# First loads of a two-layer encoder: x in blocks of 128 columns, idle products in two lists, a planner that knows two rings

## The chip, the core and the metric

The kernel runs on one core of a Trainium2 chip. The metric is device time in microseconds (us) from launch to the end of the program, taken over several runs. A core has engines that work side by side, each through its own list of instructions: TensorE (PE; PEld is its loading of stationary operands), VectorE (DVE), ScalarE (ACT), GpSimd (POOL) and SyncE (SP). SyncE and ScalarE also issue the transfers between HBM and the on-chip memory SBUF; TensorE writes its products to PSUM. An engine takes its instructions strictly in the order in which they stand, and waits at one until the semaphores that it names have come.

## What is computed

Two layers of a transformer encoder on 256 tokens of width 1024, in float32. Each layer normalises x, projects it (2560 columns), attends in three groups of heads (neighbourhood, dilated, grouped-query), normalises and projects back, and then runs a gated feed-forward part with a short convolution over tokens. Cut to what matters here (the first projection is [256, 1024] by [1024, 2560]; DEPTH is 2; q and k are normalised per head and rotated before the three attentions):

```python
def mixer_sublayer(x, n1, w_in_l, qg, kg, rpb_l, og, w_out_l, tables):
    h = rms_norm(x, n1)
    proj = h @ w_in_l
    qa, ka, va, qd, kd, vd, qc, kc, vc = jnp.split(proj, cuts, axis=-1)
    ...
    mix = jnp.concatenate([rms_norm(out_a, ...), rms_norm(out_d, ...), rms_norm(out_c, ...)], axis=-1)
    return x + mix @ w_out_l

def channel_sublayer(x, n2, w_gu, cw, cb, w_dn):
    h = rms_norm(x, n2)
    g, u = jnp.split(h @ w_gu, 2, axis=-1)
    g = depthwise_conv_centred(g, cw, cb)
    return x + (jax.nn.gelu(g, approximate=False) * u) @ w_dn

def reference(x, ...):
    for l in range(DEPTH):
        x = mixer_sublayer(x, ...)
        x = channel_sublayer(x, ...)
    return x
```

## The kernel before, in words

Products in full precision are made from halves: an operand is split into a high part (rounded to the TensorE's fast float format, `fp32r`) and a low part (what is left), and three products hi·hi, hi·lo, lo·hi are added in PSUM (`mm3`). ScalarE makes the high part (a CAST to `wp_hi`), VectorE the low part (a subtraction to `wp_lo`).

**Weights** come in units (`units_of`), each a transfer from HBM into one of four raw buffers (`wp_raw`). `load` issues it, `split` halves it. Units 0 and 1 belong to the first projection of layer 1 (dq, 384 columns): unit 0 holds rows k0 to k3 of 128, unit 1 rows k4 to k7. Unit 0 is loaded in four pieces w0 to w3 of 192 KB, unit 1 in two of 384 KB, each later one in one transfer. There are two pairs of halves (`PARTS`).

**x** lies in SBUF as 128 partitions x 2 token tiles x 1024 columns (`xs`, in the trace `const_x`). `split_T` takes two blocks of 128 columns at a time: TensorE transposes each of the two token tiles of both blocks against an identity matrix into one PSUM tile (four instructions), then ScalarE writes the high half of each block into `hT`, scaled by the norm's weights (`gains`), and VectorE the low half. So `hT` block k is needed by all products with weight rows k. `mean_squares` sums x's squares on ScalarE (four instructions of 512 columns).

**The first loads** follow the list `START` (line 44), which `load(0)` walks: which queue issues (ScalarE's or SyncE's), what ("x" a piece of x, "w" a piece of unit 0, "ident" the identity, "g" norm weights, 8 KB each), and which piece. Before, x comes in four pieces of 256 columns.

**Idle products**: 28 matmuls of a constant (`const_warm`) into a PSUM tile that nobody reads. They depend on nothing and stand in the list wherever the planner finds TensorE unoccupied.

**The order** is not that of the code. Every call goes to `Plan`, which records an operation with its cost (`cost`), the operations that it depends on, and a rank: its place in the code, plus a shift (`later(n)`). `Plan.order` then runs a model of the five engines: again and again it takes, over all engines, the operation that can begin first (ties by rank), books the engine for its cost, and hands its result on. The order that comes out is what `emit` writes, for the whole program. For a transfer the model has its own arithmetic (line 381): it begins 610 ns after its issue or when the wires are free, moves 360 bytes a ns, and is there 900 ns later. Semaphores are added afterwards: among others one that lets VectorE and ScalarE read a PSUM tile in the order in which the list has them, and one for each transfer; eight such semaphores go round, so that a ninth transfer is issued when the first has landed.

All operations carry one line of `kernel.py` in the profile, since `emit` (line 402; 408 after the change) issues every one; the tiles' names tell them apart.

Of the kernel before, what the change touches and what calls it, by code (L numbers as in the profile page):

```python
# [18 lines left out]
P = 128  # L19
# [22 lines left out]
RAWS, PARTS, AHEAD, CHUNK = 4, 2, 2, 512  # L42

START = [
    ("act", "x", 0), ("sync", "ident", 0), ("act", "g", 0), ("sync", "w", 0), ("act", "x", 1), ("sync", "w", 1),
    ("sync", "w", 2), ("sync", "w", 3), ("sync", "x", 2), ("sync", "x", 3), ("sync", "g", 1), ("sync", "g", 2),
]

WARM, WARM_W = 28, 256

# [166 lines left out]
class Plan:  # L217
# [80 lines left out]
    def order(self):  # L298
# [7 lines left out]
        free = dict.fromkeys(("PE", "ACT", "DVE", "POOL", "SP"), 550.0)  # L306
        wires = 0.0
        ready = {e: [] for e in free}
# [39 lines left out]
        while len(done) < len(ops):  # L348
            best = None
            for e, r in ready.items():  # L350
                for i in r:
                    o = ops[i]
# [28 lines left out]
            if o.method == "dma_start":  # L381
                wires = max(end + 610, wires) + o.size / 360
                end = wires + 900
            for t in o.tiles:
# [60 lines left out]
def encoder_kernel(  # L445
# [46 lines left out]

    def load_x(c, by):
        cs = slice(c * 2 * P, (c + 1) * 2 * P)
        by.dma_start(xs[:, :, cs], xv[:, :, cs])
# [10 lines left out]
    wps = psw.tile([P, WARM_W], F32, tag="w", name="wps")  # L506
    with nc.later(1000):
        for _ in range(WARM):
            nc.tensor.matmul(
                wps.rearrange("p (a b) -> p a b", b=P), warm, warm.unsqueeze(1).to_broadcast([P, WARM_W // P, P]),  # L510
                start=True, stop=True,
            )

    minus_half = const.tile([P, 32], F32, tag="mh", name="minus_half")
# [32 lines left out]
    def load(i):  # L547
# [4 lines left out]
        if i == 0:  # L552
            for by, what, c in START:
                by = nc.scalar if by == "act" else nc.sync
                if what == "w":
                    by.dma_start(rv[:, c], v[:, c])
                elif what == "x":
                    load_x(c, by)
                elif what == "ident":
                    by.dma_start(ident, c_ident)  # L560
                elif what == "g":
                    by.dma_start(gl0 if c == 0 else gl1[16 * c - 16 : 16 * c], gsrc[c])
        else:
            for c in range(0, a, 2 if i == 1 else a):
                e = c + 2 if i == 1 else a
                nc.sync.dma_start(rv[:, c:e], v[:, c:e])
# [837 lines left out]
```

## Time and profile before

| | |
|---|---|
| time, median of 3 runs (range) | 619.05 us (618.57 to 619.42) |
| the profiled execution's own time | 618.73 us |
| its span, first to last instruction | 616.9 us |
| TensorE busy | 607.5 us, 98% of the span |
| VectorE, ScalarE busy | 487.1 us, 429.8 us |
| HBM read | 102.54 MB, 169 GB/s over the span |
| TensorE busy in the first 15 us | 12.81 us |

The busy time of TensorE counts idle products as well. A matmul's shown duration is from its start to its modelled end, and successive ones overlap; how fast a row of equal ones goes is read from the start of one row to the start of the next. In rows of the timeline the first number is the start, the second the stretch from the first's start to the last's end, xN the number of equal instructions in it, and the brackets how long the engine had been idle before and for whom. In rows of windows each engine has its busy time and its number of instructions; the last three numbers are the granted clock, the busy share of the DMA engines and GB/s.

### The profile page before, as it was taken

The page shows a single profiled execution, that of the slowest core. Times are in us where ns is not written, and L with a number is a line of the kernel's source. Part 1 is how long each engine was busy: PE and PEld are TensorE (multiplying, and loading weights), DVE is VectorE, ACT ScalarE, POOL GpSimd, SP SyncE. Part 2 cuts the span into 40 slices and gives each one's busy share as a digit, 9 for nine tenths or more (in the row PEclk, how much of TensorE's full clock was granted, in tenths as well). Part 3 has the DMA queues.
Part 4 walks back from the last instruction along what each step waited for, and adds up shares of the span by engine and source line. Part 5 has one row for each costly group of instructions (what it writes and reads, how often), then busy time and mean ns, then how long its engine had stood idle before and what let it go on. Part 6 is the DMA issues. An engine that isn't in the chain of part 4 may idle for free.

```text
span 616.9 us, 9838 instructions
## 1 busy us (share of the span) xinstructions
PE 607.5 (98%) x3496; PEld 525.4 (85%) x3496; DVE 487.1 (79%) x1000; ACT 429.8 (70%) x1064; POOL 78.1 (13%) x125
## 2 busy tenths in 40 slices
PE   8999999999999999999999999999999999999997
PEld 6998888878888888888899989887888888888885
DVE  4898888897878777777867798979877777787775
ACT  6888898777565565556588899897756566556651
POOL 2732130111600000000023212112000000000000
PEclk9999999999999999999999999999999999999999
DMA  8894303466596566554444632127575565556501
GB/s 276 270 285 163 104 34 105 143 218 198 195 225 224 176 201 204 198 169 162 154 147 151 232 104 86 35 73 247 181 236 172 188 206 192 166 189 203 178 29 68
DMA packets 81345, 104.66 MB, mean 170 GB/s; under 512 B 9464, under 2 KB 68952, under 8 KB 81296
## 3 DMA queue, kind: packets, MB, share of 16 engines
q1 hardware_dynamic: 80720, 103.51, 52.0%
q8 instruction: 27, 0.44, 0.3%
q10 hardware_dynamic: 576, 0.53, 0.3%
q14 instruction: 22, 0.18, 0.1%
HBM read 102.54 MB, written 1.49 MB: 169 GB/s over the span
## 4 chain that ended last, share of the span: by engine, by line
PE 93%; ACT 3%; DVE 2%; DMA 1%; issue 1%; ACTq 0%
PE psw_w L402 49%; PE psa_a L402 44%; ACT act_s2k L402 2%; DMA const_x<-in_x_dram 1%; DVE wp_lo L402 1%; DVE act_hT L402 1%; ACT act_ch L402 0%; DVE const_x L402 0%; ACTq L402 0%; ACT wp_hi L402 0%; DVE small_nm L402 0%; ACT act_mixT_hi L402 0%; DVE act_z L402 0%; ACT act_sqm L402 0%; DVE small_rs L402 0%
## 5 line engine op out<-in xcount | busy, mean ns | idle before, releaser
L402 DVE TENSOR_TENSOR wp_lo<-wp_raw,wp_hi 128x512 fp32r<-128x512 f32 (+2 forms) x348 | 244.5, 732 | 48.2 <-ACT wp_hi L402 46.3
L402 PE MATMUL psw_w<-act_hT,wp_hi 128*128 128x512 f32 x704 | 247.8, 397 | 2.7 <-DVE act_hT L402 2.7
L402 ACT CAST wp_hi<-wp_raw 128x512 fp32r<-128x512 f32 (+2 forms) x348 | 213.0, 659 | 25.0 <-PE psw_w L402 15.7
L402 PE MATMUL psw_w<-act_hT,wp_lo 128*128 128x256 f32 x704 | 195.8, 279 | 0.0
L402 PEld LDWEIGHTS psw_w<-act_hT,wp_hi 128*128 128x128 f32 x704 | 131.9, 188 | 35.1 <-DVE act_hT L402 3.9
L402 PEld LDWEIGHTS psw_w<-act_hT,wp_lo 128*128 128x128 f32 x704 | 132.6, 188 | 1.1
L402 PE MATMUL psa_a<-wp_hi,act_hT 128*128 128x384 f32 (+2 forms) x448 | 113.4, 333 | 0.0
L402 ACT COPY act_s2k<-psw_w 128x256 f32<-128x256 f32 x88 | 32.4, 373 | 80.5 <-PE psw_w L402 80.5
L402 PEld LDWEIGHTS psa_a<-wp_hi,act_hT 128*128 128x128 f32 x448 | 78.7, 190 | 2.4
L402 PE MATMUL psa_a<-wp_lo,act_hT 128*128 128x384 f32 (+2 forms) x224 | 75.0, 335 | 0.0
L402 PE MATMUL psa_a<-wp_lo,act_ch 128*128 128x512 f32 x176 | 69.5, 395 | 0.0
L402 PE MATMUL psa_a<-wp_hi,act_ch 128*128 128x512 f32 x176 | 69.3, 394 | 0.0
L402 PE MATMUL psa_a<-wp_hi,act_cl 128*128 128x512 f32 x176 | 66.1, 394 | 0.0
L402 DVE TENSOR_TENSOR act_s2k<-psw_w,act_s2k 128x256 f32<-128x256 f32 x88 | 36.8, 422 | 30.6 <-ACT act_s2k L402 30.2
L402 PEld LDWEIGHTS psa_a<-wp_lo,act_hT 128*128 128x128 f32 x224 | 42.4, 189 | 2.0 <-DVE wp_lo L402 1.1
L402 PEld LDWEIGHTS psa_a<-wp_hi,act_cl 128*128 128x128 f32 x176 | 33.1, 188 | 7.8
L402 PEld LDWEIGHTS psa_a<-wp_hi,act_ch 128*128 128x128 f32 x176 | 33.1, 188 | 7.8
L402 PEld LDWEIGHTS psa_a<-wp_lo,act_ch 128*128 128x128 f32 x176 | 33.1, 188 | 6.9
L402 DVE SCALAR_TENSOR_TENSOR act_s2k<-act_s2k,act_cw,act_s2k 128x255 f32<-128x255 f32 x88 | 36.8, 478 | 1.4 <-ACT act_s2k L402 1.3
L402 ACT ACTIVATE act_s2k<-act_s2k,act_cw 128x256 f32<-128x256 f32 x44 | 24.1, 595 | 11.6 <-DVE act_s2k L402 11.6
L402 POOL TENSOR_TENSOR small_rstd<-small_ms,const_mh 128x6 f32<-128x6 f32 (+2 forms) x26 | 31.5, 1210 | 2.1
L402 ACT ACTIVATE act_s2k<-act_s2k 128x512 f32<-128x512 f32 x22 | 13.9, 632 | 22.4 <-DVE act_s2k L402 22.4
(109 smaller groups left out, 773.3 us busy)
## 6 DMA issues: line engine op xcount, KB each, us to landing
wp_raw<-in_w_gate_up_dram SPq DMA_DIRECT2D x44, 1024.0 KB, 5.0
wp_raw<-in_w_down_dram SPq DMA_DIRECT2D x22, 1024.0 KB, 4.9
wp_raw<-in_w_in_dram SPq DMA_DIRECT2D x14, 768.0 KB, 5.7
wp_raw<-in_w_in_dram SPq DMA_DIRECT2D x8, 1024.0 KB, 5.8
wp_raw<-in_w_out_dram SPq DMA_DIRECT2D x8, 768.0 KB, 4.3
wp_raw<-in_w_out_dram SPq DMA_DIRECT2D x4, 512.0 KB, 3.7
act_nab<-dram_scr SPq DMA_DIRECT2D x4, 448.0 KB, 7.1
out_dram<-const_x SPq DMA_DIRECT2D x4, 256.0 KB, 2.0
```

The lines of the kernel that those rows point to most:

```text
L402: getattr(o.engine.real, o.method)(*map(real, o.args), **{k: real(v) for k, v in o.kw.items()})
```

## The change

Four things. The first loads have another list: x's first two blocks of 128 columns come one by one from ScalarE's queue, the rest of x in three pieces of 256 columns from SyncE's, between pieces of unit 0; the first norm weights go from ScalarE's queue to the head of SyncE's. `load_x` takes a first block and a number of blocks. The idle products are in two lists: 13 with their own rank, 15 that are shifted by 1000 as all 28 were. And the planner's model has a ring of its own for each issuing engine, moves 150 bytes a ns for the first loads instead of 360, and lets a transfer begin 900 ns after its issue instead of 610.

```diff
 START = [
-    ("act", "x", 0), ("sync", "ident", 0), ("act", "g", 0), ("sync", "w", 0), ("act", "x", 1), ("sync", "w", 1),
     ...
+    ("act", "x", (0, 1)), ("sync", "g", 0), ("act", "x", (1, 1)), ("sync", "ident", 0), ("sync", "w", 0),
     ...
 ]
-WARM, WARM_W = 28, 256
+WARM, WARM_MORE, WARM_W = 13, 15, 256
...
-        wires = 0.0
+        wires = {}
...
             if o.method == "dma_start":
-                wires = max(end + 610, wires) + o.size / 360
-                end = wires + 900
+
+                first = i < self.first_loads
+                ring = e if first else "SP"
+                wires[ring] = max(end + 900, wires.get(ring, 0.0)) + o.size / (150 if first else 360)
+                end = wires[ring] + 900
...
-    def load_x(c, by):
-        cs = slice(c * 2 * P, (c + 1) * 2 * P)
+    def load_x(c, n, by):
+        cs = slice(c * P, (c + n) * P)
         by.dma_start(xs[:, :, cs], xv[:, :, cs])
...
-    with nc.later(1000):
-        for _ in range(WARM):
+
+    def warmed(n):
+        for _ in range(n):
             nc.tensor.matmul(
                 ...
             )
+
+    warmed(WARM)
+    with nc.later(1000):
+        warmed(WARM_MORE)
...
                 elif what == "x":
-                    load_x(c, by)
+                    load_x(*c, by)
...
+            nc.first_loads = len(nc.ops)
```

Since the model changes, the order that it writes changes too: on TensorE in about the first fifth of its list, through the first layer's mixer; from the first layer's feed-forward part on, the lists are equal again but for buffer numbers. The buffer numbers at the end of names differ between the two programs: `psa_a_154` and `psa_a_162` before, `psa_a_153` and `psa_a_160` after, are the PSUM tiles of the first projection; `wp_hi_130`, `wp_lo_140` before and `wp_hi_137`, `wp_lo_146` after are unit 0, `wp_hi_235` and `wp_hi_248` unit 1. DVE_49, Activation_49 and DMAHW0_49 to DMAHW7_49 are the semaphores of VectorE, ScalarE and the transfers.

SyncE, the first transfers, before and after:

```order
L402 DMA const_ident_81<-in_c_ident_dram 128x128
L402 DMA wp_raw_93<-in_w_in_dram 128x384 x4
L402 DMA const_x_79<-in_x_dram 128x2x256 [waits DMAHW0_49]
L402 DMA const_x_79<-in_x_dram 128x2x256 [waits DMAHW1_49]
L402 DMA act_s2k_121<-in_out_norm_g_dram 16x128 [waits DMAHW2_49]
L402 DMA act_s2k_121<-in_norm_g_dram 16x128 [waits DMAHW3_49]
L402 DMA wp_raw_138<-in_w_in_dram 128x2x384 [waits DMAHW4_49]
L402 DMA wp_raw_138<-in_w_in_dram 128x2x384 [waits DMAHW5_49]
```

```order
L408 DMA act_s2k_81<-in_norm_g_dram 16x128
L408 DMA const_ident_92<-in_c_ident_dram 128x128
L408 DMA wp_raw_96<-in_w_in_dram 128x384 x2
L408 DMA const_x_79<-in_x_dram 128x2x256
L408 DMA wp_raw_96<-in_w_in_dram 128x384
L408 DMA wp_raw_96<-in_w_in_dram 128x384 [waits DMAHW0_49]
L408 DMA const_x_79<-in_x_dram 128x2x256 [waits DMAHW1_49]
L408 DMA const_x_79<-in_x_dram 128x2x256 [waits DMAHW2_49]
L408 DMA act_s2k_131<-in_out_norm_g_dram 16x128 [waits DMAHW3_49]
L408 DMA act_s2k_131<-in_norm_g_dram 16x128 [waits DMAHW4_49]
L408 DMA wp_raw_141<-in_w_in_dram 128x2x384 [waits DMAHW5_49]
L408 DMA wp_raw_141<-in_w_in_dram 128x2x384 [waits DMAHW6_49]
```

The norm weights stand ahead of the identity; a piece of x stands among the weights; unit 1 (the two rows at the end) follows one transfer later than before.

TensorE, from the middle of unit 0, before: blocks k4 to k7 of x are transposed (two groups of four rows) while most of unit 0's products are still to come.

```order
L402 MATMUL psa_a_162<-wp_hi_130,act_hT_135 128x384
L402 LDWEIGHTS const_warm_77
L402 MATMUL psw_w_89<-const_warm_77 128x256
L402 MATMUL psa_a_154<-wp_lo_140,act_hT_135 128x384 [waits DVE_49]
L402 MATMUL psw_w_119<-const_ident_81,const_x_79 128x128 [waits DMAHW0_49]
L402 MATMUL psw_w_119<-const_ident_81,const_x_79 128x128 x3
L402 MATMUL psa_a_154<-wp_hi_130,act_hT_135 128x384
L402 MATMUL psw_w_123<-const_ident_81,const_x_79 128x128 [waits DMAHW1_49]
L402 MATMUL psw_w_123<-const_ident_81,const_x_79 128x128 x3
L402 MATMUL psa_a_154<-wp_hi_130,act_hT_135 128x384 [waits Activation_49]
L402 MATMUL psa_a_154<-wp_lo_140,act_hT_135 128x384 [waits DVE_49]
```

And after, the same two groups of four, with what stands around them:

```order
L408 MATMUL psa_a_153<-wp_lo_146,act_hT_143 128x384 [waits DVE_49]
L408 MATMUL psa_a_153<-wp_hi_137,act_hT_143 128x384
L408 MATMUL psa_a_160<-wp_lo_146,act_hT_143 128x384
L408 MATMUL psa_a_160<-wp_hi_137,act_hT_143 128x384
L408 MATMUL psw_w_121<-const_ident_92,const_x_79 128x128 [waits DMAHW1_49]
L408 MATMUL psw_w_121<-const_ident_92,const_x_79 128x128 x3
L408 MATMUL psw_w_123<-const_ident_92,const_x_79 128x128 [waits DMAHW2_49]
L408 MATMUL psw_w_123<-const_ident_92,const_x_79 128x128 x3
L408 MATMUL psw_w_89<-const_ident_92,act_s2k_131 128x32 [waits DMAHW4_49,DMAHW3_49]
L408 MATMUL psa_a_153<-wp_hi_248,act_hT_143 128x384 [waits Activation_49]
L408 MATMUL psa_a_160<-wp_hi_248,act_hT_143 128x384
```

The two groups now stand behind the last product of unit 0 and right ahead of unit 1's first.

ScalarE, from the first high halves of x to unit 1's first cast, before:

```order
L402 ACTIVATE act_hT_135<-psw_w_123,const_gains_126 128x256
L402 ACTIVATE act_s2k_150,small_ssx_149<-const_x_79 128x512 [waits DMAHW5_49,DMAHW0_49]
L402 CAST wp_hi_130<-wp_raw_93 128x384 [waits DMAHW4_49]
L402 CAST wp_hi_130<-wp_raw_93 128x384 [waits DMAHW6_49]
L402 CAST wp_hi_130<-wp_raw_93 128x384 [waits DMAHW7_49]
L402 ACTIVATE act_hT_135<-psw_w_144,const_gains_126 128x256 [waits PE_49]
L402 ACTIVATE act_hT_135<-psw_w_144,const_gains_126 128x256
L402 ACTIVATE act_s2k_190,small_ssx_149<-const_x_79 128x512
```

And after:

```order
L408 CAST wp_hi_137<-wp_raw_96 128x384 [waits DMAHW5_49]
L408 ACTIVATE act_s2k_179,small_ssx_178<-const_x_79 128x512 [waits DMAHW6_49,DMAHW2_49,DMAHW0_49]
L408 ACTIVATE act_s2k_191,small_ssx_178<-const_x_79 128x512
L408 ACTIVATE act_hT_143<-psw_w_183,const_gains_127 128x256 [waits PE_49]
L408 CAST wp_hi_137<-wp_raw_96 128x384 [waits DMAHW7_49]
L408 ACTIVATE act_hT_143<-psw_w_183,const_gains_127 128x256 [waits DVE_49]
L408 CAST wp_hi_137<-wp_raw_96 128x384 [waits DMAHW0_49]
L408 ACTIVATE act_hT_143<-psw_w_121,const_gains_127 128x256 [waits PE_49]
L408 ACTIVATE act_hT_143<-psw_w_121,const_gains_127 128x256
L408 ACTIVATE act_s2k_231,small_ssx_178<-const_x_79 128x512 [waits DMAHW2_49,DMAHW1_49]
L408 ACTIVATE act_s2k_81,small_ssx_178<-const_x_79 128x512
L408 ACTIVATE act_hT_143<-psw_w_123,const_gains_127 128x256 [waits PE_49]
```

Pieces w2 and w3 of unit 0 are no longer cast in a row but each between the high halves of x's blocks k2 and k3, and the high half of k3 waits for a result of VectorE. The last row's block and its neighbour k7 are followed by unit 1's casts.

More of the change, by code (lines that the diff above doesn't have):

```diff
@@ L44 @@
 START = [
[L45 to L46 removed]
+    ("act", "x", (0, 1)), ("sync", "g", 0), ("act", "x", (1, 1)), ("sync", "ident", 0), ("sync", "w", 0),
+    ("sync", "w", 1), ("sync", "x", (2, 2)), ("sync", "w", 2), ("sync", "w", 3), ("sync", "x", (4, 2)),
+    ("sync", "x", (6, 2)), ("sync", "g", 1), ("sync", "g", 2),
 ]
[L49 removed]
+WARM, WARM_MORE, WARM_W = 13, 15, 256
 SUM_ACT, SCALE_ACT = ("dq", "dk", "cq"), ("dk",)
```

## The prediction

> **What bounds the kernel now.** I read the shares of the page first, then the busy time by stretch, then the timeline of the first 16 us engine by engine. Busy time of the engines and the chain that ended last:
>
> ```profile
> PE 607.5 (98%) x3496; PEld 525.4 (85%) x3496; DVE 487.1 (79%) x1000; ACT 429.8 (70%) x1064; POOL 78.1 (13%) x125
> PE 93%; ACT 3%; DVE 2%; DMA 1%; issue 1%; ACTq 0%
> ```
>
> TensorE is the bound: a delay of it costs as much at the end, unless a gap further on takes it in. By stretch (first the stretch and its length, then each engine's busy time; the last numbers are the clock, DMA share and GB/s):
>
> ```profile
> 5.00:6.00 1.00, 0.96 (x5) 0.95 (x6) 0.65 (x2) 0.26 (x1) 0.00 (x0) 1.00 1.05 374
> 8.00:9.00 1.00, 1.00 (x5) 1.00 (x5) 0.64 (x3) 1.00 (x4) 0.00 (x0) 1.00 0.98 316
> 0.00:15.00 15.00, 12.81 (x68) 10.19 (x68) 6.29 (x16) 9.90 (x25) 3.70 (x14) 1.00 0.86 272
> 15.00:30.00 15.00, 15.00 (x87) 14.21 (x86) 12.09 (x27) 11.97 (x65) 11.13 (x16) 1.00 0.86 285
> 30.00:47.00 17.00, 17.00 (x109) 16.58 (x107) 15.49 (x32) 14.35 (x54) 7.19 (x16) 1.00 1.09 276
> 75.00:90.00 15.00, 14.54 (x120) 13.06 (x119) 13.56 (x33) 14.30 (x43) 5.04 (x7) 1.00 0.14 51
> 120.00:130.00 10.00, 8.67 (x50) 7.00 (x49) 9.86 (x19) 9.65 (x24) 2.20 (x4) 1.00 0.76 262
> ```
>
> From 15 us on TensorE is full, so what the change does can be read at one point: when it gets into unit 1. In the first 15 us it idles or runs idle products. The timeline there, TensorE first:
>
> ```profile
> 0.98 2.95 PE L402 MATMUL psw_w<-const_warm 128*128 128x256 bf16 x13 [0.98 <-POOL const_warm L402]
> 5.04 0.25 PE L402 MATMUL psw_w<-const_ident,act_s2k 16*128 16x16 f32 x1 [1.11 <-DMA act_s2k<-in_norm_g_dram]
> 5.23 1.11 PE L402 MATMUL psw_w<-const_ident,const_x 128*128 128x128 f32 x4
> 6.14 1.06 PE L402 MATMUL psw_w<-const_warm 128*128 128x256 bf16 x4
> 7.29 1.11 PE L402 MATMUL psw_w<-const_ident,const_x 128*128 128x128 f32 x4
> 8.06 0.67 PE L402 MATMUL psa_a<-wp_hi,act_hT 128*128 128x384 f32 x1
> 10.39 0.60 PE L402 MATMUL psw_w<-const_ident,const_x 128*128 128x128 f32 x4
> 11.01 0.60 PE L402 MATMUL psw_w<-const_ident,const_x 128*128 128x128 f32 x4
> 14.15 0.72 PE L402 MATMUL psw_w<-const_warm 128*128 128x256 bf16 x5
> 14.63 0.60 PE L402 MATMUL psa_a<-wp_hi,act_hT 128*128 128x384 f32 x2
> 15.11 0.42 PE L402 MATMUL psa_a<-wp_lo,act_hT 128*128 128x384 f32 x1
> 15.35 9.72 PE psa_a L402 x56
> ```
>
> (The last row is of the chain in order of time.) The first real product starts at 8.06, unit 1 at 14.63, its first low product at 15.11. x's blocks k4 to k7 are transposed at 10.39 and 11.01, in the middle of unit 0. ScalarE and VectorE beside it:
>
> ```profile
> 4.75 0.51 ACT L402 CAST wp_hi<-wp_raw 128x384 fp32r<-128x384 f32 x1 [1.25 <-DMA wp_raw<-in_w_in_dram]
> 6.38 0.84 ACT L402 ACTIVATE act_hT<-psw_w,const_gains 128x256 fp32r<-128x256 f32 x2 [1.12 <-PE psw_w L402]
> 7.96 1.32 ACT L402 CAST wp_hi<-wp_raw 128x384 fp32r<-128x384 f32 x3
> 9.19 0.83 ACT L402 ACTIVATE act_hT<-psw_w,const_gains 128x256 fp32r<-128x256 f32 x2
> 11.03 1.57 ACT L402 ACTIVATE act_hT<-psw_w,const_gains 128x256 fp32r<-128x256 f32 x4 [0.40 <-PE psw_w L402]
> 12.47 0.65 ACT L402 ACTIVATE act_s2k<-const_x 128x512 f32<-128x512 f32 x1
> 13.08 0.65 ACT L402 ACTIVATE act_s2k<-const_x 128x512 f32<-128x512 f32 x1
> 13.70 2.17 ACT L402 CAST wp_hi<-wp_raw 128x384 fp32r<-128x384 f32 x5
> 7.25 0.88 DVE L402 SCALAR_TENSOR_TENSOR act_hT<-psw_w,const_gains,act_hT 128x256 fp32r<-128x256 f32 x2 [1.27 <-ACT act_hT L402]
> 11.90 1.66 DVE L402 SCALAR_TENSOR_TENSOR act_hT<-psw_w,const_gains,act_hT 128x256 fp32r<-128x256 f32 x4 [0.97 <-ACT act_hT L402]
> 14.37 1.49 DVE L402 TENSOR_TENSOR wp_lo<-wp_raw,wp_hi 128x384 fp32r<-128x384 f32 x3
> ```
>
> ScalarE sets unit 1: its casts begin at 13.70, behind four high halves of x (11.03) and two sums of squares (12.47, 13.08). The loads do not. These are size and median time to landing of unit 1's two pieces and of the x piece that ScalarE issues at 1.74, and the issues of unit 1 and of the norm weights:
>
> ```profile
> wp_raw<-in_w_in_dram SPq DMA_DIRECT2D x2, 384.0 KB, 4.6
> const_x<-in_x_dram ACTq DMA_DIRECT2D x1, 256.0 KB, 5.5
> 6.18 0.42 SPq L402 DMA_DIRECT2D wp_raw<-in_w_in_dram  x1
> 7.27 0.39 SPq L402 DMA_DIRECT2D wp_raw<-in_w_in_dram  x1
> 1.23 0.48 ACTq L402 DMA_DIRECT2D act_s2k<-in_norm_g_dram  x1
> ```
>
> Issued at 6.18 and 7.27, unit 1's pieces are there by about 12, before ScalarE asks.
>
> **What one instruction takes**, from start to start: an idle product 0.22 (2.95/13) early, 0.10 late (five from 14.15 to 14.63); a transposition of x 0.23 early (5.23 to 6.14 for four), 0.11 late; a product of 384 columns 0.17 (9.72/56); a high half of x 0.36 (11.03 to 12.47 for four), a sum of squares 0.61, a cast 0.41 (7.96 to 9.19 for three); a low half of x 0.40, a low half of weights 0.48. Ends lie 0.1 later than that. PE to ACT takes 0.04 beyond the end (5.23+1.11 to 6.38), ACT to DVE 0.03 (6.38+0.84 to 7.25, and that row waits for both high halves of the pair); to PE I take 0.13.
>
> **The change, part by part.** *Loads.* The norm weights that TensorE waits for at 5.04 now head SyncE's queue, and x's first piece is half as large; the identity goes from first to second, w0 from second to third, about 0.45 later each, and unit 1 one transfer later. In exchange the first wait goes: 15 idle products from 0.98 end at 4.2, and I let the first transposition follow at 4.25 (bounds 4.2 and the 5.04 of before; 0.45 later would still be a small loss). Block 1 of x must land by 5.3 not to hold anything. Issued at 1.2, it takes between 3.8 (8 KB, issued at 1.23 and used at 5.04) and 5.5 (twice its size): 5.0 to 6.7. I take 5.3, since before it stood behind the norm weights and 256 KB and now behind 128 KB, and keep the 1.4 up to 6.7 for the range. The later loads cost nothing: the DMA engines move 316 to 374 GB/s there, unit 1 a transfer later lands by 13, and below it is wanted at 16.4: 3 us of cover, and past that each us costs one.
>
> *Start of unit 0.* From 4.25: the norm weights' transposition 0.2, two of x 0.45, two idle products 0.45, two of x 0.45 with their tail: 5.9. ScalarE makes high halves k0 and k1 from 5.95 to 6.7. TensorE's list has six idle products there, 1.3 us from 5.7: first real product at 7.0 instead of 8.06, **1.06 us earlier**.
>
> *The middle of unit 0.* This is where I see it lost. VectorE's low halves k0, k1 run from 6.8 to 7.6, then w1's low half to 8.15; TensorE, with eight products and an idle one behind it, uses it from 8.6, three more to 9.15, and only then stand the transpositions of k2 and k3: done at 9.75. ScalarE has cast w1 and done two sums of squares by 8.3 and stands idle. From 9.8 it is a chain of both engines: high k2 (9.8), cast w2 (10.15), high k3, which waits for VectorE's low k2 (10.3 to 10.77): 10.85, cast w3 (11.2 to 11.7); VectorE: low w2 10.75, low k3 11.35, low w3 11.75 to 12.3. TensorE gets w3's low half at 12.4, and its last four products take it to 13.1. Only there, by its list, come the transpositions of k4 to k7: **13.1 instead of 10.39**.
>
> *Into unit 1.* The first four take 0.45 and their tail: ScalarE's high halves k4, k5 at 13.75, 0.72; two sums of squares, 1.22, to 15.7; high halves k6, k7 (transposed long since), 0.73, to 16.43; unit 1's first cast 16.43 to 16.95; TensorE's first product of unit 1 at 17.05 instead of 14.63: **2.4 later**. And VectorE, which waits for the pair k6, k7, is at their low halves from 16.57 to 17.4, and has unit 1's first low half at 17.95: TensorE does two high products (0.35) and idles until about 18.05; before, the first low product came 0.48 behind the first high one, now 1.0. That is **0.5** more: 2.9 at this point. From here both lists are products back to back, and TensorE has no gap up to 47 us to give it back.
>
> *Idle products.* Three of the 28 stood at 70.66 to 71.1, where TensorE was full; now all stand in the first 11 us. At 0.11 each that returns **0.33**:
>
> ```profile
> 70.66 0.28 PE L402 MATMUL psw_w<-const_warm 128*128 128x256 bf16 x1
> 71.00 0.38 PE L402 MATMUL psw_w<-const_warm 128*128 128x256 bf16 x2
> ```
>
> *The rest of layer 1's order* is shuffled up to the feed-forward part. TensorE's gaps from 75 to 90 and 120 to 130 us, 0.46 and 1.33, the large ones there, are what a better order could return (1.8), and a worse one could open as much; nothing shows which, I take 0. The second layer's order is the same.
>
> Sum: 2.9 - 0.33 = 2.6. The profiled execution took 618.73 (span 616.9), so 621.3; the median 619.05 lies 0.3 above it, which makes **621.6 us**.
>
> **Rivals.** (a) *The clock is up sooner*, 0.22. The slow rate ends between the transpositions of 7.29 (0.23 each or so) and 10.39 (0.11), about 4 us after TensorE's pause of 1.11 ended at 5.04. After the change that pause is gone, so the fast rate may come by 5.6: the six idle products then take 0.6, the first real one waits for the high half k0 and comes at 6.6, and all behind it 0.4 sooner: 621.2. If the slow rate lasted to 9 us as before, the products of 384 columns ahead of w1's low half would take twice 0.17, as the transpositions take twice 0.11, and five or six of them make it up to 0.9 worse: 622.5. The Trainium skill, "TensorE: Matmul & The Clock Gate", Part 1, says that the array runs at half rate until about 3.4 us of sustained activity, counted in a free-running window: by that rule the early case holds, with the moment left to chance. The trace agrees with the order of size.
>
> (b) *The loads decide after all*, 0.10: x's last piece, on SyncE's queue behind 1.35 MB, lands after 14.4, where ScalarE's second sums of squares want it. For it: the planner's arithmetic, 1.65 MB with itself at 150 bytes a ns, from 1.9 on and 0.9 for the landing, has it at 13.8. Against: 316 to 374 GB/s in the windows above. At 16 it costs 1.5: 623.1.
>
> (c) *The new order of layer 1 gives it back*, 0.08: if the gaps of 1.8 at 75 to 130 us close, 621.6 - 1.8 = 619.8, the same as before. Against: their largest is a wait for the halves of the feed-forward part's input, which stand at a phase's end in either order (engine, tile, whom it waited for, us, times, longest):
>
> ```profile
> PEld psw_w L402 <- DVE act_hT L402: 2.0, 2, 1.6
> ```
>
> (d) *It does what its start promises*, 0.05: the gain of 1.06 at the first product is carried to the end, and the three idle products come on top: 618.7 - 1.4 + 0.3 = 617.6. It takes transpositions of k4 to k7 before ScalarE falls idle at 8.3, that is, a TensorE list other than the one shown; it decides if unit 1's casts begin before 13.2.
>
> My forecast itself has 0.55.
>
> **How the numbers follow.** A median of this kernel can tell about 0.2% (1.24 us) from no change. Forecast, (a) and (b) lie above 620.3: slower 0.87; (c) within: 0.08; (d) faster: 0.05. For the range: clock and block 1 early with half of (c)'s gaps closed, 621.6 - 0.4 - 0.9 = 620.3; block 1 late by 1.4, 623.0, or (b), 623.1; so 620.3 to 623.1.
>
> **What will show it.** In the changed profile: the first real product near 7.0; ScalarE idle between about 8.3 and 9.8 and again from 11.6 to 13.7, for TensorE's transpositions; unit 1's first cast near 16.4 with its load landed long before; TensorE idle for some 3 us ahead of unit 1, at 14 to 17 us; full from 19 to 47 us. It is wrong if the casts of unit 1 begin before 14, if they wait for a transfer, or if TensorE's gaps past 75 us change by a microsecond.

## The result, and the profile after

The changed kernel took **625.06 us** (median of 4 runs, 623.39 to 626.92), the kernel before 618.83 beside it: 1.0106 times as long, with a 95% interval of 1.0091 to 1.0121. The direction was forecast, the size was not: 2.6 us more were forecast, 6.2 measured, and the time lies outside the range of 620.3 to 623.1. The profiled execution took 624.51, its span is 622.7 (before 616.9), so the two traces differ by 5.8. One execution of the kernel before, beside the last three experiments, took 849.18 us at a granted clock of 0.657; no median and no ratio here counts it.

Busy time and the chain that ended last, and then four of the stretches shown of before (stretch and length; busy time of TensorE, its loads, VectorE, ScalarE, GpSimd; granted clock, DMA share, GB/s):

```profile
PE 608.6 (98%) x3496; PEld 526.6 (85%) x3496; DVE 487.2 (78%) x1000; ACT 429.8 (69%) x1064; POOL 75.9 (12%) x125
PE 91%; ACT 3%; DVE 3%; DMA 1%; issue 1%; POOL 1%; SPq 0%; ACTq 0%
```

```profile
15.00:30.00 15.00, 12.45 (x59) 11.65 (x59) 10.05 (x24) 10.74 (x46) 8.58 (x15) 0.89 0.73 221
30.00:47.00 17.00, 15.88 (x96) 15.77 (x97) 14.64 (x33) 13.45 (x55) 8.47 (x17) 1.00 0.90 230
75.00:90.00 15.00, 14.24 (x122) 13.15 (x121) 12.53 (x30) 13.79 (x42) 4.57 (x5) 1.00 0.28 89
120.00:130.00 10.00, 8.88 (x48) 7.33 (x47) 8.23 (x16) 6.87 (x16) 1.96 (x3) 1.00 0.61 210
```

The first two of these rows are not what was expected. From 15 to 30 us TensorE is busy for 12.45 of 15 us at a mean clock of 0.89; before, it was full, at 1.00. From 30 to 47 it lacks 1.12 us. TensorE's timeline, the rows that answer to those shown of before:

```profile
4.29 0.28 PE L408 MATMUL psw_w<-const_ident,act_s2k 16*128 16x16 f32 x1
6.48 0.44 PE L408 MATMUL psa_a<-wp_hi,act_hT 128*128 128x384 f32 x1
13.03 1.03 PE L408 MATMUL psw_w<-const_ident,const_x 128*128 128x128 f32 x8
16.90 0.62 PE L408 MATMUL psa_a<-wp_hi,act_hT 128*128 128x384 f32 x2 [2.67 <-ACT wp_hi L408]
17.88 0.44 PE L408 MATMUL psa_a<-wp_lo,act_hT 128*128 128x384 f32 x1 [0.36 <-DVE wp_lo L408]
20.31 0.52 PE L408 MATMUL psa_a<-wp_hi,act_hT 128*128 128x384 f32 x1
20.63 0.52 PE L408 MATMUL psa_a<-wp_lo,act_hT 128*128 128x384 f32 x1
31.12 0.44 PE L408 MATMUL psa_a<-wp_lo,act_hT 128*128 128x384 f32 x1 [1.41 <-DVE wp_lo L408]
```

The order did what was forecast: all eight transpositions of k4 to k7 stand in one row at 13.03, and unit 1 begins at 16.90, behind a pause of 2.67. Then come two things that were not forecast. At 20.31 the products of 384 columns follow each other by 0.32 instead of 0.17, and at 29.7 TensorE waits 1.41 for a low half of weights.

How much each costs can be read without guessing, because the products of the projections come in the same number in both kernels. The start of the same product, counted from 0, in us:

| product | before | changed | later by | what lies between |
|---|---|---|---|---|
| 0, the first | 8.06 | 6.48 | -1.58 | the new start |
| 24, unit 1's first | 14.63 | 16.90 | 2.27 | transpositions behind unit 0 |
| 32 | 16.24 | 19.03 | 2.79 | unit 1's low halves later: 0.5 |
| 48, unit 2's first | 19.02 | 23.37 | 4.35 | the stretch at half clock: 1.57 |
| 88 | 26.23 | 32.10 | 5.87 | the wait at 29.7: 1.4, and 0.1 |
| 192 | 46.90 | 52.50 | 5.60 | |
| last product with `hT` in the feed-forward part of layer 2 | 601.71 | 607.56 | 5.85 | |

**The half clock.** The clock's stretches have sharp edges in the trace, and cut there the windows show them:

```profile
15.61:19.02 3.41, 1.76 (x8) 1.44 (x9) 2.53 (x6) 3.30 (x10) 1.30 (x4) 1.00 1.05 275
19.02:22.44 3.42, 3.42 (x13) 3.42 (x12) 1.15 (x3) 1.51 (x13) 0.00 (x0) 0.50 0.97 291
22.44:26.00 3.56, 3.56 (x22) 3.56 (x22) 2.43 (x7) 3.07 (x18) 3.37 (x6) 1.00 0.44 140
```

In the 3.41 us ahead of 19.02 TensorE was busy for 1.76, about half; then the clock is at 0.50 for exactly 3.41 us, while TensorE is full, and does 13 products where the next 3.56 us hold 22.

**The wait at 29.7.** VectorE, and GpSimd beside it:

```profile
28.59 2.01 DVE L408 TENSOR_TENSOR act_sw<-act_z,act_sdq 128x48 f32<-128x48 f32 x2
30.52 0.54 DVE L408 TENSOR_TENSOR wp_lo<-wp_raw,wp_hi 128x384 fp32r<-128x384 f32 x1
28.70 1.83 POOL L408 COPY act_nab<-act_few 28x1984 f32<-28x1984 f32 x1
```

The second of two products of 48 columns takes 1.86 us (28.74 to 30.60); the first took 0.2. It began just after GpSimd's copy (28.70) and ended just after it (30.53). Behind it stands, at 30.52, the low half that TensorE waits for.

### The profile page after: what moved, and what is told of

Its sections match the earlier page's. It is cut to its first block, busy times and chain, and to the rows that moved or that the text cites. A ratio compares the mean times of both kernels' runs of the same rounds, so it can differ in the third digit from the quotient of the medians.

```text
span 622.7 us, 9840 instructions
## 1 busy us (share of the span) xinstructions
PE 608.6 (98%) x3496; PEld 526.6 (85%) x3496; DVE 487.2 (78%) x1000; ACT 429.8 (69%) x1064; POOL 75.9 (12%) x125
## 4 chain that ended last, share of the span: by engine, by line
PE 91%; ACT 3%; DVE 3%; DMA 1%; issue 1%; POOL 1%; SPq 0%; ACTq 0%
PE psw_w L408 49%; PE psa_a L408 42%; ACT act_s2k L408 2%; DMA wp_raw<-in_w_in_dram 1%; DVE wp_lo L408 1%; DVE act_hT L408 1%; ACT act_hT L408 1%; ACT wp_hi L408 0%; POOL small_rstd L408 0%; DVE const_x L408 0%; DVE act_sw L408 0%; ACT act_ch L408 0%; POOL small_ms L408 0%; SPq L408 0%; DVE act_z L408 0%
## 5 line engine op out<-in xcount | busy, mean ns | idle before, releaser
L408 PE MATMUL psw_w<-act_ch,const_v 128*128 128x256 f32 x128 | 28.7, 286 | 0.1
```

The source lines that it names most:

```text
L408: getattr(o.engine.real, o.method)(*map(real, o.args), **{k: real(v) for k, v in o.kw.items()})
```

## The experiments

Two theories go in. **The order**: the planner's 150 bytes a ns makes it believe x's last blocks late, its list puts their transpositions behind unit 0, and everything else, clock and wait included, follows from TensorE's pause there. **The loads**: smaller blocks, other queues, or idle products in two lists are themselves the cost. Splitting the idle products alone leaves every row of every engine's list where it was, with the loads and planner of before as with those of the change, so it can be neither a cost nor a gain.

### One number of the planner put back

```diff
-                wires[ring] = max(end + 900, wires.get(ring, 0.0)) + o.size / (150 if first else 360)
+                wires[ring] = max(end + 900, wires.get(ring, 0.0)) + o.size / (360 if first else 360)
```

> The changed kernel with one number of the planner put back: the first loads are planned at 360 bytes a ns instead of 150; the loads themselves, their queues and the idle products stay. Theory (the order is the cause: the planner believes x's last blocks late and so lists their transpositions behind all of unit 0): the list has the transpositions of k2 to k7 ahead of the middle of unit 0 again, unit 1's first product comes at 13.5 (13.1 to 14.2) instead of 16.91, TensorE has no pause of 2 us ahead of it, the granted clock stays full after 5.4, and the time is 617 to 620. Rival (the new loads are the cause, by small blocks or by the order of the queues): unit 1 stays at 16 or later, because ScalarE waits for a transfer, and the time stays at 623 to 627.

Measured: 618.19 us (617.38 to 619.48, 12 runs) beside 619.31, ratio 0.9979 (0.9967 to 0.9991). TensorE's timeline, and a stretch:

```profile
9.87 0.60 PE L408 MATMUL psw_w<-const_ident,const_x 128*128 128x128 f32 x4
13.31 0.61 PE L408 MATMUL psa_a<-wp_hi,act_hT 128*128 128x384 f32 x2
```

```profile
15.00:30.00 15.00, 15.00 (x88) 14.29 (x86) 12.07 (x27) 11.88 (x65) 11.38 (x15) 1.00 0.87 277
```

The last transpositions stand at 9.87, unit 1 begins at 13.31 with no wait ahead of it, 1.32 earlier than before, and TensorE is full from 15 to 30 at the full clock. With the same loads and the same idle products the change is then slightly faster than the kernel before. One number in the model made the loss.

### The planner's lines alone

```diff
...
-                wires = max(end + 610, wires) + o.size / 360
-                end = wires + 900
+                first = i < self.first_loads
+                ring = e if first else "SP"
+                wires[ring] = max(end + 900, wires.get(ring, 0.0)) + o.size / (150 if first else 360)
+                end = wires[ring] + 900
...
```

> The kernel before with only the planner's two rings and its 150 bytes a ns; loads and idle products as before. Theory (the order): the transpositions of k4 to k7 go behind unit 0 here too, unit 1's first product comes near 16.1 instead of 14.63 and its first low product near 17.1, TensorE idles about 2 us ahead of it; the time is 621 to 625, the upper part if the clock falls after that pause as it did in the changed kernel. Rival (the loads): with the loads of before the time is that of before, 618.8 within 0.6.

Measured: 623.20 us (621.40 to 624.93, 6 runs) beside 619.31, ratio 1.0060 (1.0039 to 1.0081). TensorE's timeline:

```profile
14.28 0.60 PE L404 MATMUL psw_w<-const_ident,const_x 128*128 128x128 f32 x4
16.67 0.61 PE L404 MATMUL psa_a<-wp_hi,act_hT 128*128 128x384 f32 x2 [1.62 <-ACT wp_hi L404]
```

The loads of before with the new figure: transpositions at 14.28, unit 1 at 16.67. Most of the loss comes without the new loads, 3.7 us by this ratio; why it is less than the change's 6.2 was not isolated. The rival has fallen twice. The pause of 1.62 leaves the clock full here; it falls at 30.13, behind waits of 0.62 and 1.43, the second at the same copy of GpSimd.

### The whole arithmetic of before, with the new loads

```diff
...
-                first = i < self.first_loads
-                ring = e if first else "SP"
-                wires[ring] = max(end + 900, wires.get(ring, 0.0)) + o.size / (150 if first else 360)
-                end = wires[ring] + 900
+                wires = max(end + 610, wires) + o.size / 360
+                end = wires + 900
```

> The changed kernel with the planner's whole arithmetic of the loads put back (one wire, 610 to start, 360 bytes a ns); the new loads and the two lists of idle products stay. Theory (the planner's figures alone made the loss, the loads and the idle products are a gain or nothing): unit 1's first product at 13.2 to 13.9, clock full from about 5, no pause of 2 us, time 616.5 to 619, that is 0.995 to 1.000 of the kernel before. Rival (the two rings are needed for the new loads): unit 1 after 14.6, time above the kernel before.

Measured: 617.58 us (616.91 to 619.11, 12 runs) beside 618.63, ratio 0.9985 (0.9975 to 0.9994). The new loads need no new arithmetic. The time came as expected, the trace did not: unit 1 comes at 15.62 instead of 13.2 to 13.9, because TensorE waited for a piece of x and, with a pause of 0.69 at 5.5, fell to half clock in the middle of unit 0 (the timeline, then windows cut at the clock's edges). This execution is the slowest of the 12, 619.11; when unit 1 came in the others is not on record.

```profile
8.02 1.12 PE L406 MATMUL psw_w<-const_ident,const_x 128*128 128x128 f32 x4 [1.21 <-DMA const_x<-in_x_dram]
```

```profile
4.58:7.99 3.41, 1.53 (x10) 0.90 (x8) 1.09 (x3) 1.56 (x4) 0.00 (x0) 1.00 0.96 301
7.99:11.41 3.42, 3.39 (x12) 3.38 (x13) 2.72 (x6) 3.02 (x9) 0.00 (x0) 0.50 0.98 317
```

### Figures between

Only the 150 is replaced, by 220 and by 300.

> The changed kernel, first loads planned at 220 bytes a ns, between the two. Theory (the figure decides how far the transpositions are put back): unit 1's first product at 15.1 (14.6 to 15.7), between 13.3 at 360 and 16.9 at 150, TensorE's pause ahead of it near 1.4, so that no window of 3.41 us is half idle there and the clock stays full; time 618.5 to 621. Rival (it is an either-or of one list): unit 1 at 13.3 or at 16.9.

> The changed kernel, first loads planned at 300 bytes a ns. Theory: unit 1's first product at 13.5 to 14, only 0.3 later than at 360; since at 360 about 0.9 of the start's gain was given back later, by waits that the shuffle of the rest of layer 1 decides, this may come out anywhere from 616 to 619. Rival (any lowering of the figure costs what it delays): 620 or more.

Measured: at 220, 620.12 us (619.56 to 620.73, 11 runs), ratio 1.0024 (1.0015 to 1.0033); at 300, 616.79 us (615.84 to 617.60, 6 runs), ratio **0.9968** (0.9957 to 0.9979), both beside 618.63. Unit 1's first product at 220, then at 300:

```profile
15.06 0.61 PE L408 MATMUL psa_a<-wp_hi,act_hT 128*128 128x384 f32 x2 [1.01 <-ACT wp_hi L408]
```

```profile
13.61 0.62 PE L408 MATMUL psa_a<-wp_hi,act_hT 128*128 128x384 f32 x2
```

| planned bytes a ns | unit 1's first product | ratio to the kernel before |
|---|---|---|
| 150 (the change) | 16.9 | 1.0106 |
| 220 | 15.06 | 1.0024 |
| 300 | 13.61 | 0.9968 |
| 360 | 13.31 | 0.9979 |

The start follows the figure step by step. The two last rows cannot be told apart by the start: at 300 the start's gain (1.02 at product 24) is 0.26 at product 88, partly by a TensorE wait of 0.57 at 24.2 for a low half that VectorE makes just ahead of its stall, and 2.3 at the last products. Of that, 1.4 comes between product 192 (46.62) and product 384 (133.63), and smaller gaps do not make it: those over 0.1 from 47 to 160 us add up to 1.77, before to 1.93. That this list fell out better later is luck of the shuffle, not a rule; no run isolates it. It is the fastest version here, 2 us under the kernel before.

### The pause filled, first attempt

```diff
             split_T(halves(h), hT_hi, hT_lo, 4 * h, gains[:, 0, l, 4 * h : 4 * h + 4], f"n1{l}{h}")
+        if l == 0:
+            wps = psw.tile([P, WARM_W], F32, tag="w", name="wps2")
+            with nc.not_before("PE"):
+                warmed(26)
...
```

> The changed kernel with 26 more idle products on TensorE's list, behind the transpositions of k4 to k7, where TensorE stood idle from 14.24 to 16.91. Theory (that pause dropped the clock, 19.03 to 22.44 at half, and that cost about 1.6 us): unit 1 starts at the same 16.9, the clock stays full from 5.4 on, unit 1 to 2 take 0.174 per product throughout, and the time falls by 1.6 to 623.4 (622.5 to 624.2), with less spread between runs than the 3.5 us of the changed kernel. Rival (the clock falls for another reason, the power drawn or a window that runs free of the pause): the stretch at half clock is still there and the time stays 625 or, if the idle products push unit 1 back, gets worse.

Measured: 621.95 us (620.42 to 622.60, 10 runs) beside 619.31, ratio 1.0036 (1.0023 to 1.0048): about 1.4 better than expected. The clock was full from 5.0 us on, as the theory has it, but the 26 operations had gone through the planner, and it had shuffled the rest: GpSimd's copy now ran from 24.16, and the wait at 29.7 was gone too. Unit 1 came at 17.57 instead of 16.9. So this run supports the clock's part and does not measure it. The next ones put idle products into the finished list.

### The copy moved to ScalarE

```diff
-        nc.gpsimd.tensor_copy(
+        (nc.scalar.copy if l == 0 else nc.gpsimd.tensor_copy)(
             rows_.rearrange("p (n c) -> p n c", c=RPB_C),
```

> The changed kernel with the one copy of the neighbourhood bias (28 partitions by 1984) in layer 1 on ScalarE instead of GpSimd. Theory (VectorE's small product, which took 1.86 us from 28.74 to 30.60 instead of 0.2, stood still because GpSimd's copy ran at the same time, 28.70 to 30.53, and that is TensorE's gap of 1.41 at 29.7): no such stall on VectorE, no gap at 29.7, the time about 1.4 lower, 623.6 (622.8 to 624.4). Rival (the gap is VectorE's queue being late as such after the late start): the gap stays within 0.5 of its size, the time stays at 625.

Measured: 626.42 us (624.77 to 627.07, 6 runs) beside 619.31, ratio 1.0110 (1.0092 to 1.0127): no gain. TensorE, and then GpSimd in the same trace:

```profile
37.85 0.61 PE L408 MATMUL psa_a<-wp_hi,act_hT 128*128 128x384 f32 x2 [1.29 <-ACT wp_hi L408]
39.38 0.44 PE L408 MATMUL psa_a<-wp_lo,act_hT 128*128 128x384 f32 x1 [0.74 <-DVE wp_lo L408]
33.71 1.35 POOL L408 TENSOR_TENSOR small_rstd<-small_ms,const_mh 128x6 f32<-128x6 f32 x1
```

The stall is gone and the gap of 1.41 with it (one of 0.62 at 27.3 is there), but the loss moved: free of the copy, GpSimd took five microseconds of rotation tables (27.93 to 33.26) ahead of the next norm's `small_rstd`, which it began at 33.71; ScalarE waited 2.57 for it, its casts were late, and TensorE lost 1.29 and 0.74 at 36.6 and 38.6. The clock then fell from 39.72 to 43.13. A piece of work taken off a queue is not free while a planner fills the place.

### Pause and copy, each alone and together, in the same order

Here the order stays that of the change. The copy is made small after it has been planned: it does 2 of its 64 repeats, so the kernel leaves out most of that bias, and the one row more is a clearing by GpSimd. The idle products are put in when the list is written.

```diff
+        if l == 0:
+            nc.gpsimd.memset(nabs[l].rearrange("p r c -> p (r c)")[:NR], 0.0)
...
+        if l == 0:
+            nc.ops[-1].args = (
+                rows_.rearrange("p (n c) -> p n c", c=RPB_C)[:, :2],
+                nabs["few"].unsqueeze(1).to_broadcast([NR, 2, RPB_C]),
+            )
```

```diff
                 o = self.ops[i]
+                if i == self.unit_1:
+                    w = self.ops[self.idle]
+                    for _ in range(24):
+                        w.engine.real.matmul(real(self.idle_out), *map(real, w.args[1:]), **w.kw)
...
```

> The changed kernel in exactly its order, but GpSimd's copy of the neighbourhood bias in layer 1 does 2 of 64 repeats (the rest is zero from a memset at the start; the kernel leaves out most of that bias). Theory (VectorE stands still while GpSimd copies): no VectorE instruction of 1.86 us near 28.7, TensorE's gap of 1.41 at 29.7 is gone or under 0.4, the pause of 2.67 ahead of unit 1 is as before, the time is about 1.4 below the changed kernel in the same call: near 623.6 if that one is near 625. Rival (VectorE is late there for another reason): the gap stays above 1.0 and the time stays.

> The changed kernel in exactly its order, with 24 idle products between the last transposition of x and unit 1's first product, where TensorE stood idle for 2.67 us. Theory (the pause dropped the clock): unit 1 starts at 16.9 as before, no stretch at half clock between 15 and 26, product 48 of the projections 1.6 earlier than in the changed kernel (21.8 instead of 23.4), the gap at 29.7 stays; the time is 1.6 to 2.5 below the changed kernel in the same call (its runs show one or two such stretches), 622.6 to 623.4, with a mean clock of 0.999 or 1.000. Rival (the clock falls for another reason): mean clock 0.995 to 0.997 as in the changed kernel and the same time.

> Both edits together: 24 idle products in the pause and 2 of 64 repeats of the copy. Theory: what is left is the forecast's own mechanism, the late start of unit 1 (2.8 us), less what the idle products give back: 2.6 us over the kernel before, so 621.4 to 622.2 if that is at 619. Rival (a third loss is hidden behind the two): 623 or more.

> The changed kernel again, on the same chip as the three others: 1.0106 times the kernel before, 624 to 626. Theory: runs with a mean clock of 0.997 lost one stretch of 3.41 us at half speed, those of 0.995 two, and lie about 1.7 us apart. Rival: clock and time do not go together.

Measured, all beside 618.80 us:

| | median (range), runs | ratio (95%) | mean granted clock of the runs |
|---|---|---|---|
| the change again | 625.57 (623.33 to 627.05), 6 | 1.0101 (1.0085 to 1.0117) | 0.993 to 0.999 |
| pause filled | 623.98 (622.92 to 624.64), 5 | 1.0081 (1.0069 to 1.0093) | one at 0.996, four at 0.999 and 1.000 |
| copy small | 623.27 (621.67 to 623.47), 5 | 1.0067 (1.0055 to 1.0079) | four at 0.997, one at 1.000 |
| both | 622.03 (620.54 to 623.01), 6 | 1.0051 (1.0039 to 1.0063) | all 1.000 |

The copy made small, VectorE, GpSimd and TensorE:

```profile
27.93 0.40 DVE L408 TENSOR_TENSOR act_sw<-act_z,act_sdq 128x48 f32<-128x48 f32 x2
28.04 0.23 POOL L408 COPY act_nab<-act_few 28x62 f32<-28x62 f32 x1
28.07 0.44 PE L408 MATMUL psa_a<-wp_lo,act_hT 128*128 128x384 f32 x1 [0.62 <-DVE wp_lo L408]
```

The same two products of 48 columns take 0.40 instead of 2.01, in the same place in the same list, and the wait of 1.4 is gone; the copy was the cause. A wait of 0.62 ahead of it is left. The changed kernel's first trace has none there, its second one of 0.24; both had a slow stretch ahead of the place, in which VectorE could catch up.

The pause filled, TensorE's timeline and windows:

```profile
14.62 2.79 PE L411 MATMUL psa_a<-const_warm 128*128 128x256 bf16 x24
```

```profile
27.63:31.05 3.42, 1.37 (x7) 0.88 (x6) 3.42 (x6) 0.00 (x0) 2.60 (x4) 1.00 0.01 2
31.05:34.47 3.42, 3.42 (x12) 3.42 (x12) 2.79 (x7) 1.74 (x13) 1.25 (x2) 0.50 0.56 188
```

With idle products in the pause, there is no slow stretch behind it (the clock is full from 3.75 to 31.05), and in four of five runs there is none at all. In the profiled one the clock fell later, at 31.05, behind the wait that the copy makes and the one of 0.62 ahead of it (0.62 and 1.43 in one window of 3.41). So the copy costs twice, by its wait and in some runs by the clock. The price of one slow stretch shows in the products: from product 24 to product 48 the two traces of this order with a fall there take 6.47 and 6.48, the three without (copy small, pause filled, both) 4.93, 4.92 and 4.92, so 1.55 us. Less of it is left further on, since the wait of 0.62 ahead of the copy stands in the three without the fall and is 0 and 0.24 in the two with it. The runs with the small copy (four at 0.997 took 623.25 to 623.47, one at 1.000 took 621.67) point to 1.6 to 1.8, but by a single run; in the kernel before, three runs at 0.996 and 0.997 took 618.69 to 618.87, no more than the eight others (618.49 to 620.61), and where their slow stretch lay is not on record.

By the ratios, at 618.8 us: the change costs 6.2 us; the copy's share is 2.1 with the pause open and 1.9 with it filled, the pause's share 1.2 and 1.0, both together 3.1. By the ratios' intervals each share is known to about 1.1 or 1.2 either way, so the times alone barely tell the pause's share from nothing; the products above do. What is left, 3.2 (2.4 to 3.9), holds the late start of unit 1, forecast as 2.6 with the idle products, and the wait of 0.62. One part of the expectation failed: filling the pause was to return 1.6 to 2.5 and returned 1.2. The traces fit that: 1.55 comes back by product 48, and the wait of 0.62 takes part of it. The expectation that times go by the number of slow stretches holds roughly, not exactly: in the change's runs one at 0.999 took 623.33, one at 0.997 624.61, three at 0.995 625.04 to 627.05, but one at 0.993 took 626.11, and the runs with both edits spread over 2.5 us at a clock of 1.000. Part of that spread is set in the first microseconds: the first real product starts between 6.07 and 7.06 in the five traces of this order (next section). The rest was not found.

## Why the prediction was wrong

**Right: the start, and what makes unit 1 late.** ScalarE and VectorE of the changed kernel at the places that the prediction named:

```profile
9.66 0.47 ACT L408 ACTIVATE act_hT<-psw_w,const_gains 128x256 fp32r<-128x256 f32 x1 [1.09 <-PE psw_w L408]
13.66 0.84 ACT L408 ACTIVATE act_hT<-psw_w,const_gains 128x256 fp32r<-128x256 f32 x2 [2.10 <-PE psw_w L408]
16.33 0.93 ACT L408 CAST wp_hi<-wp_raw 128x384 fp32r<-128x384 f32 x2
16.49 0.88 DVE L408 SCALAR_TENSOR_TENSOR act_hT<-psw_w,const_gains,act_hT 128x256 fp32r<-128x256 f32 x2 [0.98 <-ACT act_hT L408]
```

| step | forecast | measured |
|---|---|---|
| first transposition | 4.25 | 4.29 |
| first real product | 7.0 (rival (a): 6.6) | 6.48 |
| ScalarE goes on with k2 | 9.8 | 9.66 |
| transpositions of k4 to k7 | 13.1 | 13.03 |
| high halves k4, k5 | 13.75 | 13.66 |
| unit 1's first cast | 16.43 | 16.33 |
| low halves k6, k7 | 16.57 | 16.49 |
| unit 1's first product | 17.05 | 16.90 |
| first low product | 18.05 | 17.88 |

The chain worked out by hand from durations of the kernel before came out within 0.2 us at every step but the first product. There, rival (a)'s early clock came true (full from 5.37 instead of 8.98), but unit 1 came 0.15 sooner than forecast, not the 0.4 of (a). That the steps fit so closely is partly luck. The forecast had no term for the landing of w0, whose cast stands right ahead of the first high halves in ScalarE's list and waits for it, here in the first trace and in the second one of the changed kernel:

```profile
5.54 0.51 ACT L408 CAST wp_hi<-wp_raw 128x384 fp32r<-128x384 f32 x1 [2.53 <-DMA wp_raw<-in_w_in_dram]
6.12 0.51 ACT L408 CAST wp_hi<-wp_raw 128x384 fp32r<-128x384 f32 x1 [3.12 <-DMA wp_raw<-in_w_in_dram]
```

In the five traces of this order that cast starts between 4.79 and 6.12, the first real product between 6.07 and 7.06, and unit 1 10.40 to 10.42 later each time, at 16.48 to 17.48; the forecast had 10.05 between the two. Rival (b) fell: no wait for a transfer stands ahead of unit 1. Rival (d) named its own condition, a list other than the one shown, with unit 1's casts before 13.2; the run at 360 is such a list, and it measured 0.9979 of before where (d) had 617.6 of 619.05, 0.9977. That agreement is partly luck too: in its trace the gain of 1.32 at unit 1 is 0.62 at the last products, not carried whole as (d) had it.

**Wrong: the step "From here both lists are products back to back, and TensorE has no gap up to 47 us".** Two terms were missing behind it.

- *The clock falls back.* The prediction forecast a TensorE pause of some 3 us at 14 to 17 and let it cost its own length. It used the clock's rise in rival (a), and not its fall. Missed: 1.57 in the profiled execution (product 32 to 48).
- *VectorE is not free to run its list.* That the lists hold products back to back says nothing of how long an instruction takes. In the kernel before the same stall was there, and hidden. VectorE's list had the fourth and last low half of unit 3 ahead of the stalled product (made by 25.02), and TensorE could work through the second token tile, which needs no new one, until unit 4's first low half was made at 27.37. In the changed list that fourth low half stands behind the stalled product (30.52 in the rows above). One place in VectorE's list decided, and the other traces agree: where the fourth low half stands behind the stalled product (the changed kernel twice, the planner's lines alone, the pause filled) TensorE waits 1.41 to 1.43 there, where it stands ahead (360, 300, 220, the whole arithmetic of before) it waits 0.57 at most. The first attempt at filling the pause, with another list for TensorE too, has it behind and no such wait, so that the place decides is shown for lists alike in the rest, not for any list. Missed: 1.41 in that trace, about 2 us in the medians.

```profile
24.94 1.96 DVE L402 TENSOR_TENSOR act_sw<-act_z,act_sdq 128x48 f32<-128x48 f32 x2
24.55 2.16 POOL L402 COPY act_nab<-act_few 28x1984 f32<-28x1984 f32 x1
```

VectorE and GpSimd in the kernel before: 1.96 for two products that take 0.40 beside a small copy. The row was there to be read.

**Off in size: the rest of layer 1's order, taken at 0, and the idle products at -0.33.** The large gaps from 75 us on were 0.46, 0.14 and 1.33, and became:

```profile
88.68 0.66 PE L408 MATMUL psw_w<-const_ident,act_s2k 128*128 128x128 f32 x4 [0.76 <-ACT act_s2k L408]
129.58 0.50 PE L408 MATMUL psw_w<-act_hT,wp_hi 128*128 128x512 f32 x1 [1.12 <-DVE act_hT L408]
134.76 0.50 PE L408 MATMUL psw_w<-act_hT,wp_hi 128*128 128x512 f32 x1 [1.23 <-DVE act_hT L408]
```

That is 3.11 instead of 1.93. By the table of products the whole stretch from product 88 to the end gave back nothing net (5.87 to 5.85), where -0.33 was forecast. The gaps grew by 1.18 and the idle products return 0.33; what makes up for the remaining 0.87 was not found. Rival (c), that these gaps close, went the other way, and the prediction's own sign of being wrong, gaps past 75 us that change by a microsecond, came up.

The sum, by its own terms: unit 1 2.4, measured 2.27; its low half 0.5, measured 0.52; the half clock 0, measured 1.57; the stretch from product 48 to 88 0, measured 1.5; the rest -0.33, measured 0. With both missed terms taken out, the same order measured 622.03, 1.0051 of before, where the forecast was 621.6, 1.0041, inside the interval of 1.0039 to 1.0063; that too holds some luck, since it includes a wait of 0.62 that was not forecast. The range was too narrow because it was drawn from late loads and other gaps; what a pause of TensorE does beyond its length had no bound in it.

## What to carry to other kernels

A planner's figure for a transfer decides more than the transfer: too pessimistic (x's last piece was planned for 13.8, and in the run at 360 it is transposed at 9.87), it put six microseconds into a kernel whose loads came in time, so set such figures from landings in the trace and try some on either side. A pause of TensorE has to be priced with its clock: add up the idle time in each 3.4 us, and if about half is idle, reckon with up to half of such a stretch more for what follows (here 1.55 us at the next products, 1.0 to 1.2 in the times). When everything after a point comes later, look for stalls that the kernel before hid just there, above all VectorE instructions that take far longer than their like while GpSimd is busy.

## What was not expected of the hardware

**A pause shorter than a clock window drops the clock.** TensorE's busy time in the 3.41 us ahead of each fall was 1.76 in the changed kernel's first trace, 1.53 with the arithmetic of before, 1.37 with the pause filled, 1.39 with the planner's lines alone, 1.38 with the copy on ScalarE, and in the second trace of the changed kernel, where it fell twice:

```profile
15.66:19.07 3.41, 1.24 (x5) 0.91 (x6) 2.44 (x7) 3.41 (x11) 1.31 (x4) 1.00 1.07 264
19.07:22.49 3.42, 3.42 (x12) 3.42 (x12) 1.68 (x4) 0.97 (x8) 0.00 (x0) 0.50 0.97 297
29.32:32.73 3.41, 1.74 (x9) 1.24 (x8) 3.41 (x6) 0.00 (x0) 2.22 (x2) 1.00 0.00 0
32.73:36.14 3.41, 3.41 (x13) 3.41 (x12) 2.40 (x6) 1.74 (x13) 1.83 (x2) 0.50 0.72 231
```

Each fall lasts one window of 3.41 us, full of products, and the clock is back at once after it. With the small copy the same pause of 2.66 fell over two windows (cut by the moment the clock came up, 5.81, in steps of 3.413), busy 1.68 and 2.12, and nothing fell:

```profile
12.64:16.05 3.41, 1.68 (x13) 1.36 (x11) 0.97 (x3) 2.30 (x7) 0.17 (x1) 1.00 1.07 374
16.05:19.46 3.41, 2.12 (x10) 1.79 (x11) 2.89 (x7) 2.94 (x8) 1.14 (x4) 1.00 1.03 296
```

With the copy on ScalarE it fell over two windows as well, busy 1.79 and 2.00, and nothing fell behind them. So the bound is near half a window, and the traces do not place it closer (a fall at 1.74 and 1.76, none at 1.68 and 1.79); where the windows lie against the program changes from run to run, and with it whether a given pause costs anything. The Trainium skill, "TensorE: Matmul & The Clock Gate", "Why this matters for your kernels", advises against idle gaps above some 3 us between bursts of matmuls. By that rule the pause of 2.67 would have been harmless; in the traces it, and even 0.69 and 1.21 in one window, was followed by a whole stretch at half clock.

**A VectorE product stands still while GpSimd copies.** With the copy whole, a VectorE product of 48 columns that begins within 1 us of its start ended 0.05 to 0.1 after the copy's end: at 30.60 for 30.53 in the changed kernel, 26.79 for 26.71 before, 25.59 for 25.53 at 360 bytes a ns. With the copy small, or on ScalarE, it takes 0.2. The Trainium skill, "SBUF — State Buffer", "SBUF: two separate sides", tells of an exclusive lock on a pair of ports that VectorE and GpSimd share, held for a whole instruction, also against VectorE instructions with two inputs in SBUF where the GpSimd instruction reads SBUF. The traces agree for this copy, which reads `act_few`: the stalled products have two such inputs (`act_z`, `act_sdq`) and wait to the copy's end. They do not show it for every GpSimd instruction: in the kernel before, beside `small_rstd` (22.10 to 23.42, two inputs in SBUF), the subtraction for a low half, with two such inputs, began at 22.14 and took its usual 0.58.
